# Two scan states multiplied before either is scanned, transposes moved by two steps, small table tiles moved into the mixing phase's memory

## The chip, the cores and the metric

The kernel runs on one core of one Trainium2 chip, in fp32 (matrix products that need the accuracy are made of fp32r pairs, a high part and a low part). The metric is the device time in microseconds (us), the median of the runs shown. Engines are named as in the profile: PE multiplies matrices, DVE is the vector engine, ACT evaluates functions and copies, POOL is the general engine, SP only issues transfers.

## The reference, cut to what matters

```python
for i in range(DEPTH):                                   # DEPTH = 2, SEQ = 256, D_MODEL = 1024
    mod = (cond @ w_ada[i] + b_ada[i])[:, None, :]
    sh1, sc1, g1, sh2, sc2, g2 = jnp.split(mod, 6, axis=-1)
    h = _rmsnorm(x, norm1_g[i]) * (1.0 + sc1) + sh1
    q_a, k_a, v_a, u_s, q_r, k_r, v_r, g_r = jnp.split(h @ w_in[i], split_at, axis=-1)
    y_a = _chunk_band_attention(...)                     # softmax over a band, 8 heads
    y_s = _s5(u_s, ...)                                  # complex diagonal recurrence, below
    y_r = _retention(q_r, k_r, v_r, g_r, ...)            # 4 heads, rotary, group norm
    mixed = jnp.concatenate([y_a, y_s, y_r], axis=-1) @ w_out[i]
    x = x + g1 * mixed
    h = _rmsnorm(x, norm2_g[i]) * (1.0 + sc2) + sh2
    x = x + g2 * _hier_moe(h, ...)                       # 32 gated experts, two per token
return _rmsnorm(x, final_g)

# in _s5
dt = jnp.exp(log_dt)[:, None]
a_bar = jnp.exp(lam * dt)
bu = jnp.einsum('bsgc,gpc->bsgp', ug, b_bar)
_, states = lax.associative_scan(_linear_recurrence_combine, (a_seq, bu), axis=1)
y = jnp.real(jnp.einsum('bsgp,gcp->bsgc', states, c_mat))
```

## The kernel before, in words

Each of the two layers is a mixing phase and an expert phase, and a final norm follows.

**Mixing.** The normed input is transposed on PE (L855), scaled and shifted by the modulation (L863 to L874), and multiplied by the input weights in five products of eight k-chunks (L787 where the result is turned, L792 where it isn't). Each chunk of weights is split into two fp32r parts first: ACT copies the high part (L767), DVE subtracts it for the low part (L768). There are five buffers for split chunks, so ACT and DVE run at most five chunks ahead of PE.

Forty steps run between the chunks of the five products. A table of calls `at(step, ...)` says what each step does besides its chunk. `inner(st)` at steps 2, 10, 18 and 26 makes two states' inputs on PE (L543) in two PSUM banks with the tag `sc`, and DVE takes each state through two multiplications that read the bank (L554, L555), two half-size sums (L556, L557), two scans (L561) and two multiplications into z1 and z2 (L564, L565). The multiplications use a table E per state, which POOL makes in six instructions (L530 to L535). `outer(0)` at step 22 and `outer(1)` at step 35 multiply four states' z1 and z2 on PE (L578). States and tables share 13 buffers (`b`). The `sc` banks also hold retention's scores (L706) and attention's (L624). `ada_slot` spreads the remaining modulation products (L231, L255) over the steps; their rows are finished by DVE sums with a bias (L299 for a full row, L271 for a half row), turned on PE (L309, L285) and copied by DVE (L310, L286). Retention is rotated and normed by DVE; its variance goes through a power on POOL (L335) and three DVE instructions (L337 to L339).

PE's order is the order of the code, POOL's in mixing as well; ACT and DVE are ordered ahead of time by a scheduler that takes dependences and priorities (`high_priority`). Every engine works through its own list in order, so an instruction that waits holds up all behind it.

**The head.** Before the first layer, `s5_prep` makes radius, coefficients and the coarse and fine sine tables from [128, 16] tiles, on DVE with sines on ACT, in a pool of its own (`prep`). ACT squares x for the first norm (L343), then loads its sine table and makes the sines (L418, L419). `rms` scales x by the inverse root (L363 on DVE, L364 on ACT), and the transposes L855 read that.

**Experts.** Weights stream in by DMA through 19 slots of 1 MB; twelve rounds of experts run. `down` multiplies by the last weights (L1325) in two halves of the model width, DVE scales by the gate (L1338), `scatter` puts tokens back on PE (L1356) and DVE adds to x (L1360). In the last round (`end`) each half is scattered as soon as it is made, two token blocks each.

## Time and profile before

| | us |
|---|---|
| three runs | 843.56, 843.98, 847.43 |
| median | 843.98 |
| profiled execution, its own time | 842.86 |
| its span, first to last instruction | 841.1 |
| PE busy in it | 716.7 (85%) |
| DVE busy in it | 499.4 (59%) |
| ACT busy, POOL busy | 252.0 (30%), 112.4 (13%) |
| mean granted TensorE clock | 0.951 |

The profiled execution is the one that all rows below come from; about 1.8 us lie around its span. Busy shares are means over stages of different kinds: in the span's 40 slices of 21 us the transfers run between 413 and 420 GB/s in most slices of the expert phases, and between 141 and 382 GB/s in mixing.

### The profile page before, as it was taken

To read this page: it belongs to the slowest core of one execution; us is meant where nothing else is said; L and a number is where in the kernel's file an instruction comes from. 1 tells how busy PE (TensorE), PEld (TensorE's weight loads), DVE (VectorE), ACT (ScalarE), POOL (GpSimd) and SP (SyncE) were. 2 spreads that over 40 slices of the span, in tenths; PEclk is the share of its full clock that TensorE was granted. 3 is DMA by queue.
4 is the path that set the end of the run, shared out by engine and by line. 5 is a ranking of instruction groups with operands and counts; after the bars stand their busy time and mean duration, and the time that the engine had idled before them with its cause. 6 is when DMAs were issued, how large, how long until landed. Compare 5 with 4: busy or idle time off the path is not lost. (4 is left out here: it accounts for less than half of the span.)

```text
span 841.1 us, 12059 instructions
## 1 busy us (share of the span) xinstructions
PE 716.7 (85%) x4386; PEld 400.6 (48%) x4386; DVE 499.4 (59%) x1146; ACT 252.0 (30%) x541; POOL 112.4 (13%) x165
## 2 busy tenths in 40 slices
PE   3599979899999988598869799689989998869894
PEld 0265757675344443334227478467624344233431
DVE  4689997558555363425359989764865536252533
ACT  2343425934021121111135233394402112111112
POOL 0453160001000000000037215000000000000000
PEclk9599999999999999799999989899999999989998
DMA  9978779898999999999999754659869999989994
GB/s 372 421 269 315 272 284 340 287 376 345 417 420 415 418 416 371 389 409 419 404 413 420 280 168 141 228 216 382 324 216 420 417 415 420 414 334 414 418 411 155
DMA packets 57256, 293.66 MB, mean 349 GB/s; under 512 B 5088, under 2 KB 6880, under 8 KB 33888
## 3 DMA queue, kind: packets, MB, share of 16 engines
q1 hardware_dynamic: 54176, 288.23, 86.5%
q10 hardware_dynamic: 3008, 4.54, 1.6%
q8 instruction: 38, 0.62, 0.3%
q14 instruction: 34, 0.28, 0.1%
HBM read 289.60 MB, written 1.05 MB: 346 GB/s over the span
## 5 line engine op out<-in xcount | busy, mean ns | idle before, releaser
L1297 PE MATMUL mm<-ring,hg 128*32 128x512 f32 (+1 forms) x624 | 108.9, 595 | 0.9 <-DMA ring<-in_wgu_dram 0.9
L767 ACT ACTIVATE wh<-w 128x512 fp32r<-128x512 f32 x120 | 74.5, 630 | 98.8 <-PE mm L792 55.0
L768 DVE TENSOR_TENSOR wh<-w,wh 128x512 fp32r<-128x512 f32 x120 | 85.7, 736 | 28.3 <-ACT wh L767 27.9
L1303 DVE SCALAR_TENSOR_TENSOR b<-mm,cw,b 128x256 f32<-128x256 f32 x24 | 11.6, 483 | 141.2 <-ACT b L1301 141.2
L1297 PE MATMUL mm<-w,hg 128*64 128x512 f32 (+1 forms) x400 | 92.2, 612 | 0.0
L792 PE MATMUL mm<-wh,early 128*128 128x512 f32 x288 | 81.1, 426 | 3.7 <-DVE wh L768 3.6
L1325 PE MATMUL sc<-ring,b 128*64 128x512 f32 (+1 forms) x344 | 69.8, 597 | 1.2 <-ACT b L1311 1.1
L792 PEld LDWEIGHTS mm<-wh,early 128*128 128x128 f32 x288 | 54.7, 200 | 26.3 <-issue 6.6
L1301 ACT ACTIVATE b<-mm 128x256 f32<-128x256 f32 x24 | 9.2, 385 | 172.6 <-PE mm L1297 172.6
L1297 PEld LDWEIGHTS mm<-ring,hg 128*32 128x32 f32 (+1 forms) x624 | 30.9, 119 | 56.6 <-issue 53.3
L1343 ACT ACTIVATE y<-y 128x512 fp32r<-128x512 f32 x44 | 27.7, 629 | 92.4 <-DVE y L1338 92.4
L787 PE MATMUL mm<-early,wh 128*128 128x256 f32 x384 | 51.3, 287 | 2.5 <-DVE wh L768 2.5
L1338 DVE TENSOR_TENSOR y<-sc,gr 128x512 f32<-128x512 f32 x48 | 33.2, 692 | 32.8 <-PE sc L1325 27.0
L1275 POOL TENSOR_TENSOR b<-D,comd 128x128 f32<-128x128 f32 x32 | 12.5, 411 | 292.6 <-PE tr L1280 116.3
L1297 PEld LDWEIGHTS mm<-w,hg 128*64 128x64 f32 (+1 forms) x400 | 27.3, 134 | 50.6 <-issue 49.9
L787 PEld LDWEIGHTS mm<-early,wh 128*128 128x128 f32 x384 | 47.0, 189 | 6.4 <-DVE wh L768 3.0
L1259 PE MATMUL tr<-D,big 128*128 128x256 f32 x192 | 34.7, 323 | 16.8 <-DVE D L1210 15.4
L792 PE MATMUL mm<-wh,big 128*128 128x512 f32 x192 | 47.7, 399 | 1.4 <-DVE y L998 1.4
L231 PE MATMUL ac<-w,cc 128*32 128x512 f32 x192 | 29.1, 691 | 20.3 <-DVE cc L225 10.7
L1259 PEld LDWEIGHTS tr<-D,big 128*128 128x128 f32 x192 | 29.1, 217 | 25.6 <-issue 20.4
L1345 DVE TENSOR_TENSOR y<-y,y 128x512 fp32r<-128x512 f32 x44 | 30.3, 689 | 17.8 <-ACT y L1343 17.5
L792 PEld LDWEIGHTS mm<-wh,big 128*128 128x128 f32 x192 | 35.0, 188 | 9.3 <-DVE y L998 2.2
(367 smaller groups left out, 1161.6 us busy)
## 6 DMA issues: line engine op xcount, KB each, us to landing
ring<-in_wgu_dram SPq DMA_DIRECT2D x78, 1024.0 KB, 16.5
w<-in_wgu_dram SPq DMA_DIRECT2D x50, 1024.0 KB, 14.5
w<-in_w_ada_dram SPq DMA_DIRECT2D x36, 1024.0 KB, 9.1
ring<-in_moe_w_down_dram SPq DMA_DIRECT2D x36, 1024.0 KB, 19.9
w<-in_win_dram SPq DMA_DIRECT2D x22, 1024.0 KB, 7.7
w<-in_moe_w_down_dram SPq DMA_DIRECT2D x20, 1024.0 KB, 17.4
ring<-in_w_ada_dram SPq DMA_DIRECT2D x12, 1024.0 KB, 7.9
w<-in_w_out_dram SPq DMA_DIRECT2D x8, 1024.0 KB, 7.2
```

The source lines that it names most:

```text
L231: PE.matmul(acc[32 * t:32 * t + 32, :], c1[:, k:k + 1].to_broadcast([128, 32]), w[:, t * 512:(t + 1) * 512], start=(k == 0), stop=(k == 7) ...
L767: A.activation(wh[:, 0], w, AF.Copy)
L768: lo_eng[par_[0] % len(lo_eng)].tensor_tensor(wh[:, 1], w, wh[:, 0].bitcast(F32), op=ALU.subtract)
L787: PE.matmul(pt[t][:, f * 256:(f + 1) * 256], whs[i][:, w_, fs], a[x_][:, k], start=first and f + m == 0, stop=end and m == 2, skip_group_c ...
L792: PE.matmul(pt[t], a[x_][:, k, ts_], whs[i][:, w_], start=first and m == 0, stop=end and m == 2)
L1259: PE.matmul(pc[c], (xlo if i else xhi)[:, t, cs], Dm[blk][:, t, ss], start=(i + t == 0), stop=(i + t == 3))
L1275: G.tensor_tensor(Dc[:, t].rearrange("p (e s) -> p e s", s=w), Dm[blk][:, t, po:po + 128].bitcast(F32).rearrange("p (e s) -> p e s", s=w), ...
L1297: PE.matmul(gu[o:o + w, :], hg[blk, k][:, po + o:po + o + w], ws[k // 4][j][:, k % 4] if ahead else part_gu(l, es[j], k), start=(k == 0), ...
L1325: PE.matmul(yp[h][o:o + w, :], aT[:, f * 128 + o:f * 128 + o + w], wd[h][f][j] if ahead else part_wd(l, es[j], f, h), start=(f == 0), stop ...
L1338: V.tensor_tensor(y, yp[h], gates[l, 2][:, h * 512:(h + 1) * 512], op=ALU.mult)
L1343: A.activation(yh, y, AF.Copy)
L1345: V.tensor_tensor(yl, y, yh.bitcast(F32), op=ALU.subtract)
```

## The change

Six edits, the computation is the same:

1. `inner` issues L554 and L555 of both states ahead of either state's scan; `scan` starts from their results.
2. Tables come at step `4*st-6` instead of `4*st-4`. On POOL, whose order is the code's, one thing moves in each layer: the second power of retention (L335) stands behind the table of state 6, where it stood ahead of it.
3. `half_biased` (L285) runs at `g+3` instead of `g+1`, and the sums L271 (of the half row that is turned) and L299 get high priority.
4. `s5_prep` runs in layer 0's mixing phase, its small tiles are slices of one `y2` tile, and an `early` tile that nothing used is gone. `first_squares` copies a column of the cosines into the squares' scratch bank first (one DVE copy more, the only instruction that is new), so ACT's first squares come behind the first sines.
5. `gate_up` gives its activation and product high priority; no instruction changes place by that.
6. In the last round of each layer, the first half's two scatters stand behind the second half's first and second quarter of L1325, where both stood ahead of the second half.

```diff
         def half_slot(l, i):
...
-                V.tensor_tensor(row, acc[:, 0:256], bias_row.pop((l, 2)), op=ALU.add)
+                with tc.high_priority(offset=PRIO):
+                    V.tensor_tensor(row, acc[:, 0:256], bias_row.pop((l, 2)), op=ALU.add)
...
         def ada_gate(l, acc):
...
-            V.tensor_tensor(row, acc, bias_row.pop((l, 1)), op=ALU.add)
+            with tc.high_priority(offset=PRIO):
+                V.tensor_tensor(row, acc, bias_row.pop((l, 1)), op=ALU.add)
...
+        small = []
+
+        def s16():
+
+            if not small:
+                t = y2([128, 512])
+                small.extend(t[:, i * 16:(i + 1) * 16] for i in range(32))
+            return small.pop(0)
...
             sincos(sn, cs, ph, hf)
-            between()
+            between(cs)
...
             def inner(st0):
...
+                ms = []
                 for i, bu in enumerate(bus):
-                    scan(st0 + i, bu)
-
-            def scan(st, bu):
+                    E = E_[st0 + i]
+                    m1 = b2([128, 2, 256])
+                    m2 = b2([128, 2, 256])
+                    with tc.high_priority(offset=PRIO):
+                        V.tensor_tensor(m1, bu, E[:, 0, None, :].to_broadcast([128, 2, 256]), op=ALU.mult)
+                        V.tensor_tensor(m2, bu, E[:, 1, None, :].to_broadcast([128, 2, 256]), op=ALU.mult)
+                    ms.append((m1, m2))
+                for i, m in enumerate(ms):
+                    scan(st0 + i, *m)
+
+            def scan(st, m1, m2):
...
-                        at(4 * st - 4 + i, tables, st + i)
+                        at(max(4 * st - 6, 0) + i, tables, st + i)
...
                     if j == 11:
-                        at(g + 1, lambda: half_biased(l, ada_acc[l, 2]))
+                        at(g + 3, lambda: half_biased(l, ada_acc[l, 2]))
...
-                    if end and (f, j) == (1, len(es) - 1):
-
-                        ys = outputs(yp, True, (h,))
-                        scatter(end, ys, h)
+                    if end and j == len(es) - 1:
+
+                        if f == 1:
+                            ye[h] = outputs(yp, True, (h,))
+                        if h == 1:
+                            scatter(end, ye[0], 0, (f,))
+                            if f == 1:
+                                scatter(end, ye[1], 1)
...
-        with phase("prep"):
-            s5_prep(lambda: all_squares(ss0, ps("mm")))
+
+        def first_squares(cs):
+
+            scr = ps("mm")
+            V.tensor_copy(scr[:, 0:1], cs[:, 0:1])
+            all_squares(ss0, scr)
+
         for l in range(L):
             more = l + 1 < L
             with phase("mix"):
-
-                early()
+                if l == 0:
+                    s5_prep(first_squares)
                 xn = early().rearrange("p (t d) -> p t d", t=2)
```

Line numbers shift by the edit: what stands at L285, L299, L363, L554, L555, L556, L557, L561, L564, L565, L578, L624, L714, L768 and L792 before stands at L286, L301, L365, L562, L563, L571, L572, L576, L579, L580, L593, L639, L729, L783 and L807 in the change.

DVE in the head, before: `early` is the scaled x that the first transposes read, `crs_c` the coarse cosine table, `co_im` a coefficient.

```order
110 L472 TENSOR_TENSOR co_im<-m2t_211,m_36_210 128x16
111 L413 SCALAR_TENSOR_TENSOR b_45_250<-b_46_251,b_45_250 128x256
112 L414 TENSOR_SCALAR b_45_250<-b_45_250 128x256
113 L420 TENSOR_TENSOR b_46_251<-b_46_251 128x256
114 L421 TENSOR_SCALAR crs_c<-b_46_251 128x256
115 L363 TENSOR_SCALAR early_272<-x,rry_280 128x512 x2
```

The same place of the change, up to the scaling of x:

```order
93 L340 SCALAR_TENSOR_TENSOR rrt_248<-rrt_248,ssv_243 128x2
94 L467 TENSOR_TENSOR y_11_111<-y_11_111 128x16
95 L466 SCALAR_TENSOR_TENSOR y_11_111<-y_11_111 128x16
96 L341 SCALAR_TENSOR_TENSOR rry_246<-rrt_248,rry_246 128x2
97 L477 TENSOR_TENSOR y_11_111<-y_11_111,cst 128x16
98 L476 TENSOR_TENSOR y_11_111<-y_11_111,cst 128x16
99 L365 TENSOR_SCALAR early_238<-x,rry_246 128x512 x2
100 L478 TENSOR_TENSOR y_11_111<-y_11_111 128x16
```

The scaling of x stood behind the whole chain of the coarse table and now follows the inverse root (`rry`) at once.

DVE in layer 1, second pair of states, before: `sc` is the bank with a state's input, `y<-ac,bad` the sum L299 of a modulation row, `y<-sc,cst` retention's masked scores.

```order
890 L554 TENSOR_TENSOR b_1837_6604<-sc_6598,b_1809_6494 128x512
891 L555 TENSOR_TENSOR b_1838_6605<-sc_6598,b_1809_6494 128x512
892 L299 TENSOR_TENSOR y_1851_6668<-ac_6210,bad_6211 128x512
893 L556 TENSOR_TENSOR b_1837_6604<-b_1837_6604,b_1838_6605 128x256
894 L557 TENSOR_TENSOR b_1837_6604<-b_1837_6604,b_1838_6605 128x256
895 L310 COPY modT_96<-tr_6695 128x16
896 L561 SCALAR_TENSOR_TENSOR b_1838_6605<-radius,b_1837_6604 128x256 x2
897 L564 TENSOR_TENSOR b_1839_6612<-b_1838_6605,b_1809_6494 128x512
898 L554 TENSOR_TENSOR b_1840_6615<-sc_6599,b_1813_6509 128x512
899 L555 TENSOR_TENSOR b_1841_6616<-sc_6599,b_1813_6509 128x512
```

The same pair in the change:

```order
888 L562 TENSOR_TENSOR b_1807_6569<-sc_6563,b_1775_6433 128x512
889 L563 TENSOR_TENSOR b_1808_6570<-sc_6563,b_1775_6433 128x512
890 L562 TENSOR_TENSOR b_1809_6573<-sc_6564,b_1780_6457 128x512
891 L563 TENSOR_TENSOR b_1810_6574<-sc_6564,b_1780_6457 128x512
892 L301 TENSOR_TENSOR y_1824_6642<-ac_6175,bad_6176 128x512
893 L571 TENSOR_TENSOR b_1807_6569<-b_1807_6569,b_1808_6570 128x256
```

The second bank is read two rows behind the first instead of eight, and the sum of the row stands two full-size multiplications later.

PE in layer 1 near the end of the products, before: `tr<-cst,y` is the turning of the half row, `mm<-wh,early` the products, `sc<-b,b` attention's first scores, `ac<-b,par` and `ac<-b,b` are `outer(1)`.

```order
2086 L792 MATMUL mm_7207<-wh_7231,early_6279 128x512
2087 L285 MATMUL tr_7240<-cst,y_1942_7229 128x128 x2
2088 L792 MATMUL mm_7206<-wh_7244,early_6278 128x512 x2
2089 L792 MATMUL mm_7206<-wh_7244,early_6279 128x512
2090 L792 MATMUL mm_7207<-wh_7244,early_6278 128x512 x2
...
2092 L624 MATMUL sc_7253<-b_1789_6407,b_1788_6406 128x256
```

The change, at the end of `outer(1)`, which stands behind those scores:

```order
2112 L593 MATMUL ac_6929<-b_1856_6812,par_6190 32x256
2113 L593 MATMUL ac_6929<-b_1890_7040,par_6190 32x256
2114 L593 MATMUL ac_6929<-b_1892_7044,par_6190 32x256
2115 L286 MATMUL tr_7265<-cst,y_1912_7194 128x128 x2
2116 L807 MATMUL mm_7171<-wh_7271,early_6243 128x512 x2
```

The turning moved behind two chunks of the last product, the scores and `outer(1)`. In layer 0 it moved less: behind 18 products (L787) and one turning of retention (L748 twice).

## Rows read from the trace of the kernel before

**Rows 1.** The page: busy time by engine, and transfer rate in 40 slices.

```profile
PE 716.7 (85%) x4386; PEld 400.6 (48%) x4386; DVE 499.4 (59%) x1146; ACT 252.0 (30%) x541; POOL 112.4 (13%) x165
...
GB/s 372 421 269 315 272 284 340 287 376 345 417 420 415 418 416 371 389 409 419 404 413 420 280 168 141 228 216 382 324 216 420 417 415 420 414 334 414 418 411 155
```

**Rows 2.** Windows, layer 1: busy PE, PEld, DVE, ACT, POOL; PEclk, DMA share, GB/s.

```profile
480.00:490.00 10.00, 6.59 (x22) 4.82 (x23) 9.82 (x18) 1.38 (x4) 5.87 (x8) 0.75 0.55 207
...
500.00:510.00 10.00, 10.00 (x111) 8.23 (x108) 8.52 (x26) 2.18 (x5) 2.82 (x4) 1.00 0.53 184
510.00:520.00 10.00, 9.51 (x75) 8.61 (x75) 10.00 (x16) 4.88 (x8) 8.64 (x10) 1.00 0.49 150
```

**Rows 3.** Timeline of PE, the head: start, duration, work, [idle before <- releaser].

```profile
24.88 1.93 PE L231 MATMUL ac<-w,cc 128*32 128x512 f32 x8 [0.55 <-DMA w<-in_w_ada_dram]
29.68 1.97 PE L855 MATMUL sc<-cst,early 128*128 128x128 f32 x8 [2.87 <-DVE early L363]
```

**Rows 4.** Timeline of DVE, the head.

```profile
20.45 0.15 DVE L339 SCALAR_TENSOR_TENSOR rry<-rrt,rry 128x2 f32<-128x2 f32 x1
...
28.69 1.71 DVE L363 TENSOR_SCALAR early<-x,rry 128x512 f32<-128x512 f32 x2
```

**Rows 5.** Timeline of PE and of DVE, layer 0 near the half row.

```profile
116.81 1.57 PE L787 MATMUL mm<-early,wh 128*128 128x256 f32 x11 [1.98 <-DVE wh L768]
...
125.05 0.44 PE L285 MATMUL tr<-cst,y 128*128 128x128 f32 x2 [2.98 <-DVE y L271]
...
124.57 0.42 DVE L271 TENSOR_TENSOR y<-ac,bad 128x256 f32<-128x256 f32 x1
```

**Rows 6.** Timeline of PE and of DVE, layer 1, second pair of states.

```profile
485.36 1.64 PE L706 MATMUL sc<-y,y 64*128 64x256 f32 x6 [3.10 <-DVE b L555]
486.94 5.29 PE L792 MATMUL mm<-wh,early 128*128 128x512 f32 x12
...
484.63 0.68 DVE L555 TENSOR_TENSOR b<-sc,b 128x512 f32<-128x512 f32 x1
```

**Rows 7.** Timeline of PE and of DVE, layer 1, end of the scans.

```profile
532.12 1.42 PE L792 MATMUL mm<-wh,early 128*128 128x512 f32 x5 [0.77 <-DVE wh L768]
539.02 0.69 PE L285 MATMUL tr<-cst,y 128*128 128x128 f32 x2 [5.48 <-DVE y L271]
539.36 2.91 PE L792 MATMUL mm<-wh,early 128*128 128x512 f32 x6
542.20 1.32 PE L624 MATMUL sc<-b,b 64*128 64x256 f32 x8
...
545.04 1.07 PE L578 MATMUL ac<-b,par 128*32 128x256 f32 x16
...
537.95 0.68 DVE L565 TENSOR_TENSOR b<-b,b 128x512 f32<-128x512 f32 x1
```

**Rows 8.** Timeline of POOL and of DVE, layer 1, table of state 6.

```profile
508.20 1.11 POOL L335 TENSOR_TENSOR rvy<-rvar,mhalf 128x4 f32<-128x4 f32 x1 [5.71 <-DVE rvar L735]
509.28 0.62 POOL L530 TENSOR_TENSOR b<-crs_c,fine_c 128x256 f32<-128x256 f32 x1
...
513.86 0.99 POOL L535 TENSOR_TENSOR b<-b,b 128x256 f32<-128x256 f32 x1
...
509.34 0.57 DVE L337 TENSOR_TENSOR rvt<-rvy 128x4 f32<-128x4 f32 x1 [0.90 <-POOL rvy L335]
...
517.02 1.11 DVE L768 TENSOR_TENSOR wh<-w,wh 128x512 fp32r<-128x512 f32 x1
```

**Rows 9.** Timeline of PE, end of layer 0, start and end of layer 1.

```profile
437.90 1.94 PE L855 MATMUL sc<-cst,early 128*128 128x128 f32 x8 [1.47 <-DVE early L363]
...
825.18 1.98 PE L1356 MATMUL ac<-y,sT 128*128 128x512 f32 x4 [0.81 <-DVE y L1338]
827.09 1.92 PE L1325 MATMUL sc<-ring,b 128*32 128x512 f32 x16
829.90 1.98 PE L1356 MATMUL tr<-y,sT 128*128 128x512 f32 x4 [0.89 <-DVE y L1338]
```

More of the change, by code (lines that the diff above doesn't have):

```diff
@@ L373, in body @@
         COEF = [1.0 / 5040, 1.0 / 720, 1.0 / 120, 1.0 / 24, 1.0 / 6, 0.5, 1.0]
+        small = []
[4 more added lines that the diff above has]
+            return small.pop(0)
         def expm1(src, w, tag):
-            xx = sb([128, w], tag + "x")
+            xx = s16()
             V.tensor_scalar(xx, src, -87.3, 88.0, op0=ALU.max, op1=ALU.min)
-            n = sb([128, w], tag + "n")
+            n = s16()
             round_(n, xx, 1.4426950408889634)
@@ L382, in expm1 @@
             V.scalar_tensor_tensor(xx, n, -LN2L, xx, op0=ALU.mult, op1=ALU.add)
-            q = sb([128, w], tag + "q")
+            q = s16()
             V.tensor_scalar(q, xx, 1.0 / 40320, COEF[0], op0=ALU.mult, op1=ALU.add)
@@ L392, in expm1 @@
             p2 = ni.bitcast(F32)
-            em1 = sb([128, w], tag + "em1")
+            em1 = s16()
             V.tensor_tensor(em1, q, p2, op=ALU.mult)
-            pm1 = sb([128, w], tag + "pm1")
+            pm1 = s16()
             V.tensor_scalar(pm1, p2, -1.0, None, op0=ALU.add)
             V.tensor_tensor(em1, em1, pm1, op=ALU.add)
-            ex = sb([128, w], tag + "ex")
+            ex = s16()
             V.tensor_scalar(ex, q, 1.0, None, op0=ALU.add)
@@ L433, in s5_prep @@
             _, dt = expm1(ldt, 16, "e1")
-            live = sb([128, 16], "live")
+            live = s16()
             V.tensor_scalar(live, ldt, -87.3, None, op0=ALU.is_ge)
             V.tensor_tensor(dt, dt, live, op=ALU.mult)
-            zr = sb([128, 16], "zr")
+            zr = s16()
             V.tensor_tensor(zr, C("are"), dt, op=ALU.mult)
-            phi = sb([128, 16], "phi")
+            phi = s16()
             V.tensor_tensor(phi, C("aim"), dt, op=ALU.mult)
-            n = sb([128, 16], "pn")
-            ph = sb([128, 16], "ph")
+            n = s16()
+            ph = s16()
             mod2pi(ph, phi, n)
@@ L445, in s5_prep @@
             V.tensor_copy(radius, ex)
-            sn = sb([128, 16], "psn")
-            cs = sb([128, 16], "pcs")
-            hf = sb([128, 16], "phf")
+            sn = s16()
+            cs = s16()
+            hf = s16()
             sincos(sn, cs, ph, hf)
-            between()
-            nr = sb([128, 16], "nr")
-            ni = sb([128, 16], "nni")
+            between(cs)
+            nr = s16()
+            ni = s16()
             V.tensor_tensor(nr, em1, cs, op=ALU.mult)
@@ L456, in s5_prep @@
             V.tensor_tensor(ni, ex, sn, op=ALU.mult)
-            m2 = sb([128, 16], "m2")
-            t = sb([128, 16], "m2t")
+            m2 = s16()
+            t = s16()
             V.tensor_tensor(m2, C("are"), C("are"), op=ALU.mult)
@@ L463, in s5_prep @@
             V.reciprocal(m2, m2)
-            t2 = sb([128, 16], "m2t2")
+            t2 = s16()
             V.tensor_tensor(t, nr, C("are"), op=ALU.mult)
@@ L472, in s5_prep @@
             V.tensor_tensor(co_im, t, m2, op=ALU.mult)
-            ph16 = sb([128, 16], "ph16")
+            ph16 = s16()
             V.tensor_scalar(phi, ph, 16.0, None, op0=ALU.mult)
             mod2pi(ph16, phi, n)
-            t16 = sb([128, 16], "t16")
+            t16 = s16()
             V.tensor_scalar(t16, C("iota")[:, 0:16], -1.0, None, op0=ALU.add)
@@ L544, in inner @@
                                   tile_position=(o, 0))
+                ms = []
                 for i, bu in enumerate(bus):
-                    scan(st0 + i, bu)
-            def scan(st, bu):
+                    E = E_[st0 + i]
[8 more added lines that the diff above has]
+            def scan(st, m1, m2):
                 q = l * 8 + st
                 E = E_.pop(st)
-                m1 = b2([128, 2, 256])
-                m2 = b2([128, 2, 256])
-                with tc.high_priority(offset=PRIO):
-                    V.tensor_tensor(m1, bu, E[:, 0, None, :].to_broadcast([128, 2, 256]), op=ALU.mult)
-                    V.tensor_tensor(m2, bu, E[:, 1, None, :].to_broadcast([128, 2, 256]), op=ALU.mult)
                 V.tensor_tensor(m1[:, 0], m1[:, 0], m2[:, 1], op=ALU.subtract)
@@ L1299, in gate_up @@
                               start=(k == 0), stop=(k == 7), tile_position=(0, o))
-                si = b1_([128, 256])
-                A.activation(si, gu[:, 0:256], AF.Silu)
-                act = b1_([128, 256])
-                V.scalar_tensor_tensor(act, gu[:, 256:512], cw, si, op0=ALU.mult, op1=ALU.mult)
+                si, act = b1_([128, 256]), b1_([128, 256])
+                with tc.high_priority(offset=PRIO):
+                    A.activation(si, gu[:, 0:256], AF.Silu)
+                    V.scalar_tensor_tensor(act, gu[:, 256:512], cw, si, op0=ALU.mult, op1=ALU.mult)
                 return act
@@ L1315, in down @@
                 _, _, w, _, _, es = rounds[r]
-                yp = [ps("sc") for _ in range(2)]
+                yp, ye = [ps("sc") for _ in range(2)], {}
                 if ahead and end:
@@ L1347, in outputs, with scatter @@
                 return out
-            def scatter(sT, ys, h0=0):
+            def scatter(sT, ys, h0=0, ts=(0, 1)):
                 for h, (yh, yl) in enumerate(ys, h0):
                     hs = slice(h * 512, (h + 1) * 512)
-                    for t in range(2):
+                    for t in ts:
                         p = ps(("ac", "tr")[h])
```

## The prediction

> **What bounds the kernel now.** I read the page first. PE is busy for 85% of the span and DVE for 59% [rows 1], but these shares mix stages, so the transfer rate in 40 slices comes next: it stands at 413 to 420 GB/s through most of the expert phases and falls to 141 to 382 in mixing [rows 1]. The expert phases go at the pace of the weights; mixing doesn't. The windows of layer 1's mixing show what it goes by: from 500 to 510 us PE is busy for all of 10.00 us, from 510 to 520 DVE is, and from 480 to 490 DVE is busy for 9.82 while PE has 6.59 and a granted clock of 0.75 [rows 2]. So PE and DVE take turns, and a microsecond is to be had only where PE stands still for DVE. The timeline of PE names these places. In the head PE waits 2.87 us for the scaled x [rows 3]. In layer 0 it waits 1.98 and 2.98 us [rows 5], in layer 1 3.10 us [rows 6], 0.77 and 5.48 us [rows 7]. At the end two scatters lie between the halves of the last round [rows 9].
>
> What is saved in mixing should reach the end, since the expert phases' transfers start as slots and routing allow, not by a clock of their own: in the two slices from 589 to 631 us, around the end of layer 1's mixing, the rate is 324 and 216 [rows 1], so transfers wait there for the core.
>
> **The head (term A).** Before, DVE had the inverse root of the norm by 20.60 (20.45 + 0.15) but scaled x only at 28.69, behind the chain of the coarse cosines [rows 4]. Now the scaling follows the root. What is late next is PE itself: the modulation product that stands ahead of the transposes ends at 26.81 (24.88 + 1.93) [rows 3]. The transposes go from 29.68 to about 26.85: **A = 2.8 us**. The squares now come behind the first sines and the one new copy. Even if they pushed the root back by 4 us, the scaling (1.71) would end at 20.60 + 4 + 1.71 = 26.3, ahead of 26.85; so that costs nothing, and each microsecond beyond 4.5 would cost one. POOL's tables get their coarse tables later by at most the scaling's 1.71 from a chain that otherwise starts earlier, and nobody waits for them in the head.
>
> **Layer 0's mixing (B0).** The half row's turning waited 2.98 us for its sum at 124.57 [rows 5]. The turning now stands 18 products and two transposes later; 11 products took 1.57 [rows 5], so 18 take about 2.6, and even with the sum no earlier the wait would be 0.4. The 1.98 ahead of it is a wait for a split chunk (L768) behind a state's multiplications and scan. DVE has no less work, only another order, so this may return at the next chunk. Bounds: 2.6 us if all of it returns, 4.96 if none does. **B0 = 3.3**, nearer the lower end, since DVE is fully busy there as in the like window of layer 1 (10.00 of 10) [rows 2].
>
> **Layer 1's mixing (B1).** Two places. The first: retention's scores need a bank that the second state's L555 frees; that ended at 485.31 (484.63 + 0.68), and PE waited 3.10 for it [rows 6]. Now the bank is read two rows behind the first one, and that wait goes. The sum L299 falls behind two multiplications more of 0.68 each [rows 6], so the turning L309 waits up to 1.4 more. Net 1.7. The 12 products behind it took 5.29 us, at a mean clock of 0.75, a mix of its two levels of 1.2 and 2.4 GHz [rows 2, 6]; six at the full clock take 1.7 (1.42 for five) [rows 7], so 12 take 3.4, and up to 1.9 more comes back if the clock stays up.
>
> The second: the turning that waited 5.48 now stands behind `outer(1)`. It can't wait again, as the sum it needs stands in DVE's list ahead of the last state's L565, which `outer(1)` needs. What is late next is that L565: it ended at 538.63 (537.95 + 0.68), while `outer(1)` began at 545.04 [rows 7]. PE, let go at 533.54 (532.12 + 1.42), has 12 products (3.4) and the scores (1.32) to do: 538.3 [rows 7]. Both allow a start near 539.2 with some queueing, 5.8 earlier, even if DVE is not a microsecond ahead of before. The slow 2.91 for six products after the stall [rows 7] is part of these 5.8.
>
> The 1.7 (or 3.6) of the first place helps the second only if DVE gets ahead too, and from 510 to 520 it has no idle time [rows 2] but for what came before: 0.90 us behind POOL's power [rows 8]. So of the first place I keep 0.5. **B1 = 6.3**. Bounds: 3, if the splits of the last product come later by half of the stall; 9.4, if the first place passes whole (5.8 + 3.6).
>
> **The ends (C0, C1).** In layer 1 the second half's products started at 827.09, behind the first half's scatters, and its own scatter at 829.90 [rows 9]. Now the first eight products run while DVE scales the first half (PE waited 0.81 for that [rows 9]); one scatter block (0.99) stands ahead of the second eight and one behind. PE's own work is unchanged (1.92 + 1.98 until the last scatter), so it gains its wait of 0.81 and the wait of 0.89 at 829.90 that the other block now covers: **C1 = 1.5**, at most 1.7, at least 0.8. The same edit in layer 0 can only shorten the wait of 1.47 for the scaled x at 437.90 [rows 9], where the transfers of the modulation weights set the pace otherwise: **C0 = 0.4** of 0 to 1.47.
>
> **What costs nothing.** POOL's order changes only at retention's second power, which now stands behind a table of 5.6 us (509.28 to 514.85) [rows 8]. The table waits for buffers of `outer(0)`, the power for the table, DVE's L337 for the power, and behind L337 stand splits that PE needs. But DVE's list has 13 instructions between the variance and L337 where it had one; six are full-size at up to 0.68 [rows 7], four are scans, which I put at the same, and three half-size, at half: 7.8, which covers the table and the power of 1.11 [rows 8] with 1 us to spare. The high priority in the expert rounds moves nothing. The memory of the small tiles takes away a wait at most.
>
> **Sum.** 2.8 + 3.3 + 6.3 + 1.5 + 0.4 = 14.3 us. The profiled execution took 842.86, so 828.6; the median of the runs is 1.1 above it, 843.98, so I forecast **829.7 us**.
>
> **Rivals.**
>
> *The waits come back as waits for splits.* DVE's work is the same, and it has windows without idle time [rows 2]; PE then only waits elsewhere. Against it: in layer 1 `outer(1)` stood 6.4 us behind the DVE result that it needs (545.04 less 538.63) [rows 7], and that is not DVE's work. Half of B0 and B1 lost gives 829.7 + 4.8 = 834.5; all but A, C1 and the 2.6 of B0 lost gives 843.98 - 6.9 = 837.1.
>
> *Layer 0's saving is lost in the transfers.* If weights for the first expert phase arrive no earlier, A and B0 vanish: 829.7 + 6.1 = 835.8. For it speaks that the rate is 376 and 345 in the slices from 168 to 210 us [rows 1], against it that these are below the 417 to 420 of the slices that follow.
>
> *POOL in DVE's way.* A split that ran beside the table took 1.11 us (517.02) where DVE's other full-size instructions there take 0.68 [rows 7, 8]. The table of 5.6 us starts about 1.1 earlier now, as the power no longer stands ahead of it. Were it and the next one, in both layers, moved whole from idle to busy DVE time, that would be 5 instructions of 0.43 more each per table, 2.2, and 8.6 over four: 838.3. I see only 1.1 us of shift, so this is unlikely. The Trainium skill says it as a rule (GPSIMD Engine Reference, Key points): POOL shares its SBUF interfaces with the vector engine and contends with vector instructions that have two SBUF inputs. The trace's 1.11 agrees.
>
> *Slower: POOL's power holds DVE.* If `outer(0)` comes late, because PE itself waits for splits, the table, the power and L337 slip with it, and DVE stops with the splits behind L337. Each microsecond by which `outer(0)` slips past the 1 us of cover costs one in each layer. It eats the whole gain when the slip is 14.3 / 2 + 1 = 8.2 us; a slip of 10 gives 829.7 + 18 = 847.7. Against it: PE was busy for 10.00 of 10 us around `outer(0)` in layer 1 [rows 2], so nothing made it late.
>
> **How the numbers follow.** My forecast, 825 to 834, gets 0.70; the waits that come back, 834 to 838, 0.13; lost in the transfers 0.06; POOL in the way 0.03; no gain at all for a cause I don't see 0.04; slower 0.04. The lower end takes the upper bounds of B0, B1 and C1 together in part (4.96 + 9.4 + 1.7 + 2.8 + 0.4 = 19.3 gives 824.7, and all at once is unlikely); the upper end takes in the rivals that still gain: 825 to 839. Half a per cent, about what can be told from no change, is 4.2 us, so faster means under 839.8: 0.70 + 0.13 + 0.06 and nearly all of POOL's 0.03 make 0.91, and I take 0.89 as the cases' own ends reach over. Same 0.07, slower 0.04.
>
> **What would show it.** In the changed profile: the first transposes near 26.9 us behind a modulation product, with no wait for DVE (A); no wait at the half row's turning in either layer, and `outer(1)` of layer 1 within 1 us of the last L565 (B0, B1); no wait at retention's scores, and a longer one at L309 in layer 1; a last scatter about 1.5 us nearer to the second half's first product. Wrong it would be if the windows of 10 us show PE's waits for L768 grown by what the others lost, if DVE waits several microseconds for POOL's second power, or if the first weights of the expert phases land as late as before.

## The result and the profile after

The changed kernel took 823.83 us, median of four runs (822.90 to 825.42), beside 843.81 before: the ratio is 0.9768, with a 95% interval of 0.9746 to 0.9789, so about 20 us or 2.3% less. The forecast was 829.7 with a range down to 825.0: the side was right, the size 30% short, and the time lies below the range.

The page of the changed kernel, lines as in [rows 1]; its span is 821.1 us:

```profile
PE 711.6 (87%) x4386; PEld 397.6 (48%) x4386; DVE 491.4 (60%) x1147; ACT 251.8 (31%) x541; POOL 114.4 (14%) x165
...
GB/s 369 420 371 303 291 344 291 295 335 416 414 422 414 419 416 359 399 412 417 406 409 420 336 189 145 288 259 316 300 314 421 415 417 418 401 350 412 419 410 154
```

Most slices of the expert phases stand at the rates that they had before, and most of the 20 us is gained in the head and in mixing. To see where, one follows PE through both traces: its list is the same but for a few places, so the start of one instruction before, less its start after, is the lead that the change has at that place.

| place on PE | before | after | lead | forecast of the step |
|---|---|---|---|---|
| first scan inputs, layer 0 (L543) | 54.78 | 49.46 | 5.3 | A, 2.8 |
| third scan inputs, layer 0 (L543) | 95.68 | 87.84 | 7.8 | none (it was 2.5) |
| attention's first scores, layer 0 (L624) | 139.31 | 132.39 | 6.9 | B0, 3.3 (0.9 lost since the row above, 1.6 in all) |
| first turning of the scans' input matrices, layer 1 (L504) | 448.74 | 440.27 | 8.5 | C0, 0.4 (it was 1.5) |
| retention's first turning, layer 1 (L695) | 474.96 | 463.60 | 11.4 | none (it was 2.9) |
| `outer(0)`, layer 1 (L578) | 506.86 | 493.32 | 13.5 | 0.5 of B1 (2.2 since the row above, 5.1 in all) |
| `outer(1)`, layer 1 (L578) | 545.04 | 523.39 | 21.7 | 5.8 of B1 (it was 8.1) |
| first expert round's turning, layer 1 (L1309) | 616.89 | 597.11 | 19.8 | none (1.9 given back) |
| end of the span | 841.1 | 821.1 | 20.0 | C1, 1.5 (it was 0.2) |

The head, PE (compare [rows 3]); columns of every timeline below are start, duration, work and [idle before <- releaser], lines of the code as in the changed kernel:

```profile
24.73 1.68 PE L231 MATMUL ac<-w,cc 128*32 128x512 f32 x8 [0.55 <-DMA w<-in_w_ada_dram]
26.33 1.09 PE L870 MATMUL sc<-cst,early 128*128 128x128 f32 x8
27.26 0.60 PE L870 MATMUL tr<-cst,early 128*128 128x128 f32 x4
27.70 0.60 PE L870 MATMUL mm<-cst,early 128*128 128x128 f32 x4
```

The transposes follow the modulation product with no wait, as forecast. What was not forecast: the first eight take 1.09 us where they took 1.97.

Layer 0, retention's first scores and the bank that they wait for, PE of the kernel before and then of the changed kernel:

```profile
81.56 1.71 PE L706 MATMUL sc<-y,y 64*128 64x256 f32 x8
```

```profile
75.57 0.92 PE L721 MATMUL sc<-y,y 64*128 64x256 f32 x8
```

This is the place of [rows 6], one layer earlier. Before, the bank came free with DVE's L555 at 82.24 (81.56 and 0.68), in the middle of the eight. The next scores went from 1.41, with a wait of 0.54 ahead of them, to 0.92, and a wait of 0.61 for a split (at 71.57) went too. Together that is about the 2.5 of the table. It is edit 1's: with edit 1 alone both groups of scores take 0.92, in the whole without it 1.71 and 1.40.

Layer 0 near the half row, PE and DVE (compare [rows 5]):

```profile
115.84 0.44 PE L286 MATMUL tr<-cst,y 128*128 128x128 f32 x2 [0.98 <-DVE y L272]
...
119.47 0.69 PE L763 MATMUL tr<-cst,b 128*128 128x128 f32 x2 [2.19 <-DVE big L769]
119.81 6.12 PE L802 MATMUL mm<-early,wh 128*128 128x256 f32 x30
...
115.38 0.41 DVE L272 TENSOR_TENSOR y<-ac,bad 128x256 f32<-128x256 f32 x1
```

The wait of 1.98 fell to 0.19 (at 107.23) and that of 2.98 to 0.98, and one of 2.19 came where none was: retention's second turning (L763) needs the bank that DVE's L769 reads, and the half row's turning now stands between the two and holds the other bank. The 30 products behind it took 6.12 us; before they took 3.84.

The granted clock stands beside both places in the windows (columns as in [rows 2]; the third column from the end is the clock, 1.00 being 2.4 GHz and 0.50 being 1.2). The kernel before, the head's transposes and the 30 products:

```profile
31.00:32.00 1.00, 1.00 (x7) 1.00 (x6) 0.00 (x0) 0.00 (x0) 0.94 (x2) 0.50 1.00 418
...
119.00:122.00 3.00, 3.00 (x34) 1.95 (x30) 3.00 (x6) 0.05 (x1) 0.00 (x0) 1.00 0.85 307
```

The changed kernel, the same two:

```profile
27.00:28.00 1.00, 1.00 (x11) 1.00 (x10) 0.00 (x0) 0.00 (x0) 1.00 (x2) 1.00 0.98 410
...
120.00:123.00 3.00, 3.00 (x16) 3.00 (x16) 3.00 (x9) 1.39 (x4) 0.00 (x0) 0.50 1.03 415
```

The head came up from the lower level to the upper one, and the products near the half row went the other way.

Layer 1, second pair of states, PE (compare [rows 6]):

```profile
471.00 1.09 PE L311 MATMUL tr<-cst,y 128*128 128x128 f32 x4 [3.13 <-DVE y L301]
471.74 1.63 PE L807 MATMUL mm<-wh,early 128*128 128x512 f32 x3
473.30 1.65 PE L721 MATMUL sc<-y,y 64*128 64x256 f32 x8
474.88 3.81 PE L807 MATMUL mm<-wh,early 128*128 128x512 f32 x12
```

The scores no longer wait for their bank, and the row's turning waits 3.13 in place of 1.08. The 12 products behind take 3.81 in place of 5.29.

Just ahead of this, before and then after:

```profile
469.48 1.43 PE L792 MATMUL mm<-wh,early 128*128 128x512 f32 x5 [1.85 <-DVE wh L768]
...
472.37 2.75 PE L792 MATMUL mm<-wh,early 128*128 128x512 f32 x6
```

```profile
459.67 1.44 PE L807 MATMUL mm<-wh,early 128*128 128x512 f32 x5 [0.55 <-DVE wh L783]
...
462.10 1.66 PE L807 MATMUL mm<-wh,early 128*128 128x512 f32 x6
```

A wait for a split fell by 1.30, and the scan inputs and the six products behind it took 1.13 and 1.66 in place of 1.60 and 2.75. That makes about the 2.9 of the table. The wait goes with edit 1: it is 0.54 with edit 1 alone, and 1.85 in the whole without it.

Layer 1, end of the scans, PE and DVE (compare [rows 7]):

```profile
521.80 1.66 PE L807 MATMUL mm<-wh,early 128*128 128x512 f32 x6
523.39 1.10 PE L593 MATMUL ac<-b,par 128*32 128x256 f32 x15
...
525.50 0.44 PE L286 MATMUL tr<-cst,y 128*128 128x128 f32 x2
...
523.35 0.68 DVE L580 TENSOR_TENSOR b<-b,b 128x512 f32<-128x512 f32 x1
```

Here `outer(1)` runs right at the last state's L580 (L565 before): that ends at 524.03, 14.6 us earlier than before, and PE no longer stands 6.4 us behind it.

### The profile page after: what moved, and what is told of

The parts are those of the page before. It is cut to its first block, busy times and chain, and to the rows that moved or that the text cites. A ratio compares the mean times of both kernels' runs of the same rounds, so it can differ in the third digit from the quotient of the medians.

```text
span 821.1 us, 12064 instructions
## 1 busy us (share of the span) xinstructions
PE 711.6 (87%) x4386; PEld 397.6 (48%) x4386; DVE 491.4 (60%) x1147; ACT 251.8 (31%) x541; POOL 114.4 (14%) x165
## 5 line engine op out<-in xcount | busy, mean ns | idle before, releaser
L783 DVE TENSOR_TENSOR wh<-w,wh 128x512 fp32r<-128x512 f32 x120 | 85.2, 733 | 25.4 <-ACT wh L782 24.9
L807 PE MATMUL mm<-wh,early 128*128 128x512 f32 x288 | 77.3, 411 | 0.9 <-DVE wh L783 0.9
L807 PEld LDWEIGHTS mm<-wh,early 128*128 128x128 f32 x288 | 52.4, 192 | 22.0 <-issue 6.3
L802 PE MATMUL mm<-early,wh 128*128 128x256 f32 x384 | 53.2, 295 | 1.6 <-DVE wh L783 1.6
L802 PEld LDWEIGHTS mm<-early,wh 128*128 128x128 f32 x384 | 49.3, 198 | 5.4 <-DVE wh L783 2.0
L807 PE MATMUL mm<-wh,big 128*128 128x512 f32 x192 | 47.6, 398 | 1.4 <-DVE y L1013 1.4
L807 PEld LDWEIGHTS mm<-wh,big 128*128 128x128 f32 x192 | 35.0, 188 | 9.2 <-DVE y L1013 2.2
## 6 DMA issues: line engine op xcount, KB each, us to landing
w<-in_wgu_dram SPq DMA_DIRECT2D x50, 1024.0 KB, 14.3
```

The source lines that it names most:

```text
L783: lo_eng[par_[0] % len(lo_eng)].tensor_tensor(wh[:, 1], w, wh[:, 0].bitcast(F32), op=ALU.subtract)
L802: PE.matmul(pt[t][:, f * 256:(f + 1) * 256], whs[i][:, w_, fs], a[x_][:, k], start=first and f + m == 0, stop=end and m == 2, skip_group_c ...
L807: PE.matmul(pt[t], a[x_][:, k, ts_], whs[i][:, w_], start=first and m == 0, stop=end and m == 2)
```

## The experiments

Each was timed beside runs of the kernel before on the same chip. Gains in us are (1 - ratio) times 843.8, so 19.6 for the whole change.

| kernel | median, us | ratio (95% interval) | gain, us |
|---|---|---|---|
| before + 4 (head) | 837.47 | 0.9939 (0.9917 to 0.9960) | 5.1 |
| before + 1 (multiplications ahead) | 848.94 | 1.0067 (1.0049 to 1.0085) | -5.7 |
| before + 3 (turning later, row sums first) | 838.96 | 0.9957 (0.9943 to 0.9972) | 3.6 |
| before + 6 (last round) | 842.47 | 0.9990 (0.9971 to 1.0010) | 0.8, not told from none |
| before + 1 + priority of L299 | 841.38 | 0.9968 (0.9953 to 0.9983) | 2.7 |
| before + 1 + 3 | 832.06 | 0.9864 (0.9849 to 0.9879) | 11.5 |
| before + matmuls of no use in the head | 844.99 | 1.0015 (0.9998 to 1.0032) | -1.3, not told from none |
| after - 1 | 832.51 | 0.9867 (0.9842 to 0.9892) | 11.2 |
| after - priority of L299 | 829.91 | 0.9830 (0.9812 to 0.9848) | 14.3 |
| after - 2 (tables at the old steps) | 827.22 | 0.9812 (0.9797 to 0.9826) | 15.9 |
| after + two turnings later | 820.52 | 0.9714 (0.9692 to 0.9737) | 24.1 |
| after + retention's second turning later | 818.87 | 0.9704 (0.9687 to 0.9720) | 25.0 |

**The head alone.** Edit 4 was put into the kernel before, with the small tiles that it needs; its core:

```diff
-        with phase("prep"):
-            s5_prep(lambda: all_squares(ss0, ps("mm")))
...
-                early()
+                if l == 0:
+                    s5_prep(first_squares)
```

> The kernel before with edit 4 alone (small tiles in the mixing phase, first squares behind the first sines). Theory from the two traces: the head gains the wait of 2.8 us and about 2.4 more because PE's clock is at its upper level for the transposes, so 5 us in all: 838.8. Rival, as the prediction has it: only the wait, 2.8: 841.0. Rival, lost later in transfers or in waits for DVE: 843.8, no change.

It gained 5.1 us: the wait and the clock. In its trace PE is 4.3 ahead at the first scan inputs (54.78 to 50.53) and 6.3 at the end (841.1 to 834.8), so the rival that it is lost in the transfers falls.

**Multiplications ahead, alone.** Edit 1 was put into the kernel before, with nothing else:

```diff
-                    scan(st0 + i, bu)
...
+                    ms.append((m1, m2))
+                for i, m in enumerate(ms):
+                    scan(st0 + i, *m)
```

> The kernel before with edit 1 alone (both states' first multiplications ahead of either scan). Theory: the wait at retention's scores in layer 1 goes, the clock stays up and DVE follows, 4 to 5 us: 839. Rival, as the prediction has it: DVE has no idle time at the end of the scans, so only 0.5 of it stays: 843.3. In both the turning of the half row in layer 1 still waits, 5 us or more.

Neither: it is slower by 5.7 us. In its trace the wait at the scores is gone, and the turning of the full row waits, PE of layer 1:

```profile
478.47 0.94 PE L796 MATMUL mm<-wh,early 128*128 128x512 f32 x3
488.95 1.08 PE L309 MATMUL tr<-cst,y 128*128 128x128 f32 x4 [9.54 <-DVE y L299]
```

With both states' multiplications first, the sum L299, which has no priority there, falls behind both states' scans on DVE. In layer 0 the edit alone loses too: the half row's turning waits 4.20 (2.98 before) and a split 2.78 (1.98 before).

**Turning later and row sums first, alone.** Edit 3 was put into the kernel before, the two priorities (of L271 and L299) and the later step:

```diff
-                        at(g + 1, lambda: half_biased(l, ada_acc[l, 2]))
+                        at(g + 3, lambda: half_biased(l, ada_acc[l, 2]))
```

> The kernel before with edit 3 alone (the half row turned two steps later, the two row sums at high priority). Theory from the traces: layer 1's turning gives 8, with the slow products behind it, less 2 given back in attention, layer 0 gives 1 to 2: 836.5. Rival, as the prediction has it: 5.8 and 2.6, 835.4. Rival, the edit is worth something only with edit 1: under 3 us, 841 or more.

It gained 3.6, between the theories. The turnings of the half row wait no more than 0.30 us in layer 0 and not at all in layer 1, but the scores still wait 2.60 and retention's second turning of layer 0 waits 2.6.

**The last round alone.** Edit 6 was put into the kernel before:

```diff
+                        if f == 1:
+                            ye[h] = outputs(yp, True, (h,))
+                        if h == 1:
+                            scatter(end, ye[0], 0, (f,))
```

> The kernel before with edit 6 alone (the last rounds' scatters between the quarters). Theory from the trace: the last weights land when they did, and the last scatter stands 3.1 us behind them where it stood 3.4: 0.3 to 0.5, 843.4. Rival, as the prediction has it: 1.5 and 0.4, 841.9.

0.8 us with an interval over zero. The trace of the changed kernel shows what it ends on. Windows of half a microsecond, before and then after; the last three columns are PE clock, DMA share and GB/s:

```profile
826.50:827.00 0.50, 0.50 (x2) 0.00 (x0) 0.50 (x1) 0.00 (x0) 0.00 (x0) 1.00 0.15 57
827.00:827.50 0.50, 0.50 (x5) 0.16 (x8) 0.47 (x2) 0.38 (x1) 0.00 (x0) 1.00 0.00 0
```

```profile
806.50:807.00 0.50, 0.50 (x2) 0.00 (x0) 0.00 (x0) 0.00 (x0) 0.00 (x0) 1.00 0.24 90
807.00:807.50 0.50, 0.50 (x4) 0.15 (x6) 0.19 (x1) 0.00 (x0) 0.00 (x0) 1.00 0.04 16
```

```profile
807.20 1.55 PE L1340 MATMUL sc<-ring,b 128*32 128x512 f32 x8
808.68 1.12 PE L1375 MATMUL ac<-y,sT 128*128 128x512 f32 x2
809.64 1.88 PE L1375 MATMUL tr<-y,sT 128*128 128x512 f32 x4
```

Before, the second half's products began at 827.09, just as the last weights were in (827.0); their transfer had hidden behind the scatters. After, the last eight products begin at 807.20, again just as the last weights are in (807.2). So it is the weights that set this place in both, and only the work behind them is shorter: the last scatter starts 2.4 us behind the end of the transfers (809.64 less 807.2) where it was 2.9 (829.90 less 827.0).

**The whole without edit 1.** Each state's scan stands behind its own multiplications again:

```diff
-                for i, m in enumerate(ms):
-                    scan(st0 + i, *m)
+                    scan(st0 + i, bu)
```

> The changed kernel without edit 1 (each state's scan behind its own multiplications again). Theory: edit 1 is worth much once the row sums have priority, since then the bank is free early and the sum isn't late: without it the single edits add up to 843.8 - 5.1 - 3.6 - 0.8, about 834. Rival, as the prediction has it: little of edit 1 stays, 825 to 826.

832.51: with the others in place, edit 1 is worth 8.4 us (19.6 less 11.2). Alone it cost 5.7.

**Edit 1 with one priority.** To the kernel before:

```diff
+            with tc.high_priority(offset=PRIO):
-            V.tensor_tensor(row, acc, bias_row.pop((l, 1)), op=ALU.add)
+                V.tensor_tensor(row, acc, bias_row.pop((l, 1)), op=ALU.add)
```

> The kernel before with edit 1 and the high priority of the full row's sum L299 alone. Theory: what made edit 1 alone slower by 5.7 us is that this sum falls behind both states' scans, so that the turning L309 waits 9.5 us in layer 1; with the priority it waits about 3, and edit 1 then gains its 3 to 5 at the scores and the clock: 841 to 843. Rival: the loss is the half row's or the buffers', 848.

841.38: these two lines turn edit 1 from 5.7 slower to 2.7 faster. The full row's turning waits 3.13 in layer 1. In layer 0 the half row's turning, whose sum has no priority here, still waits 4.55.

**Matmuls of no use in the head.** They were put on PE between the modulation products and ahead of the transposes of the kernel before.

```diff
+                    hot = ps("ac")
                     for k in range(7):
                         ada_mm(acc0, k, ada0[k])
+                        for _ in range((0, 0, 0, 1, 1, 1, 5)[k]):
+                            PE.matmul(hot[:, 0:256], ident, cst[:, 0:256], start=True, stop=True)
```

> The kernel before with eight matmuls of no use in the head, which keep PE busy between the modulation products and up to the first transposes; nothing else is moved and no result changes. Theory: 2.4 of the head's 5.3 us are the clock, so the transposes (1.97, 1.06, 1.06) take 1.09, 0.60 and 0.60 and the product behind them 1.06 of 1.62, 2.2 us in all: 841.6. Rival: the upper level was chance, or PE falls behind by these matmuls: 843.8 or more.

The end is no earlier, but the rows tell the two questions apart, PE and then DVE:

```profile
25.64 2.42 PE L840 MATMUL ac<-cst 128*128 128x256 f32 x10
29.82 1.09 PE L858 MATMUL sc<-cst,early 128*128 128x128 f32 x8 [1.76 <-DVE early L363]
30.75 0.60 PE L858 MATMUL tr<-cst,early 128*128 128x128 f32 x4
31.18 0.60 PE L858 MATMUL mm<-cst,early 128*128 128x128 f32 x4
...
42.24 0.80 PE L885 MATMUL mm<-early,wh 128*128 128x256 f32 x2 [8.09 <-ACT early L876]
...
33.99 4.08 DVE L768 TENSOR_TENSOR wh<-w,wh 128x512 fp32r<-128x512 f32 x4 [3.47 <-ACT wh L767]
38.00 0.16 DVE L317 TENSOR_TENSOR modT<-tr,cst 128x16 f32<-128x16 f32 x1
```

The transposes take 1.09, 0.60 and 0.60 as in the changed kernel, although x still comes late, and the next turning (L316) starts 3.68 us behind them, where it was 5.96. The clock there, in a window of this kernel:

```profile
30.00:31.00 1.00, 1.00 (x11) 1.00 (x11) 0.53 (x1) 0.22 (x1) 0.92 (x2) 1.00 1.02 424
```

So 2.3 us there are the clock. They were lost behind it: with the matmuls in PE's list the scheduler put the four splits L768 ahead of the modulation on DVE, and the first product waits 8.09. As a test of the end time it is confounded.

**Two turnings later.** The changed kernel with

```diff
-                        at(g + 1, lambda: ada_biased(l, 1, ada_acc[l, 1]))
+                        at(g + 1 + 2 * l, lambda: ada_biased(l, 1, ada_acc[l, 1]))
...
-                at(29, rout, 1)
+                at(32, rout, 1)
```

> The changed kernel with two turnings moved: the full row's of layer 1 by two steps (it waited 3.13 us for its sum) and retention's second by three (2.19 in layer 0, and 30 products behind it took 6.12 us of 3.84). Theory: both waits go and the clock stays up, 3 to 6 us: 819. Rival: DVE has no idle time there and PE waits for splits in their place: 823.

820.52. In layer 1 its lead over the changed kernel is 5.4 at `outer(0)` (493.32 to 487.97), and 1.1 at `outer(1)` (523.39 to 522.31); it had 1.5 when layer 1 began (445.58 to 444.04). So there all that layer 1 had added was lost again, in one new wait on PE, for a bank that ACT frees; ACT's list is shown behind it:

```profile
497.01 7.31 PE L802 MATMUL mm<-early,wh 128*128 128x256 f32 x36 [3.22 <-ACT b L967]
...
496.06 0.42 ACT L755 ACTIVATE b<-r 128x256 f32<-128x256 f32 x1 [8.77 <-DVE rvar L749]
```

L967, which frees the bank, stands right behind L755 on ACT, and L755 waited 8.77 us for retention's variance on DVE (2.87 in the changed kernel). From 490 to 500 us of this kernel DVE is busy for 10.00 of 10. So PE had got ahead of DVE, and waited for it by way of ACT.

**Retention's second turning alone.** The changed kernel with

```diff
-                at(29, rout, 1)
+                at(32, rout, 1)
```

> The changed kernel with only retention's second turning moved by three steps. Theory: in layer 0 the wait of 2.19 and the slow 30 products behind it go, 4 us, and this is nearly all of what the two moves together gave, as layer 1's lead of 5 was down to 1 at the second outer product: 820 to 821. Rival: the lead of layer 0 doesn't reach the end, and the gain was layer 1's: 823.

818.87, the lowest median here, though its interval overlaps with that of the two moves together. The 30 products of layer 0 take 3.85 again, and nothing waits at L763:

```profile
117.34 3.85 PE L802 MATMUL mm<-early,wh 128*128 128x256 f32 x30
...
123.61 0.38 PE L763 MATMUL tr<-cst,b 128*128 128x128 f32 x2
```

**Edits 1 and 3, nothing else.** The kernel before with both of the diffs above.

> The kernel before with edits 1 and 3 together and nothing else. Theory: the two need each other, so together they give what of the changed kernel's 20 us the head (5.1) and the last round (0.8) leave: about 830. Rival, each is worth what it is alone (5.7 slower, 3.6 faster): 846.

832.06: 11.5 us, where the two alone give 3.6 - 5.7 = -2.1. So 13.6 of the change's 19.6 us are in the pair and in neither one. In its trace the half row's turning of layer 0 waits no more, which had waited 4.20 with edit 1 alone.

**The whole without the priority of L299.**

```diff
-            with tc.high_priority(offset=PRIO):
-                V.tensor_tensor(row, acc, bias_row.pop((l, 1)), op=ALU.add)
+            V.tensor_tensor(row, acc, bias_row.pop((l, 1)), op=ALU.add)
```

> The changed kernel without the high priority of the full row's sum L299 alone. Theory: the sum falls behind both states' scans, the turning L309 of layer 1 waits 8 to 10 us where it waits 3.1, and PE's products behind it are slow: 830 to 832. Rival: the lead is taken back by DVE's full list at the end of the scans in any case, so little is lost: 824 to 825.

829.91, 5.3 us lost. PE waits 9.6 us at the full row's turning in layer 1.

**The whole with the tables at their old steps.**

```diff
-                        at(max(4 * st - 6, 0) + i, tables, st + i)
+                        at(4 * st - 4 + i, tables, st + i)
```

> The changed kernel with the tables at their old steps, so that retention's second power stands ahead of the table of state 6 again. As the prediction has it, the earlier tables cost and bring nothing: 823 to 825. Rival: the power behind the table holds DVE up, so that this is faster, 821. Rival: the earlier table is what lets the third pair of states start, 827 or more.

827.22, so edit 2 is worth 3.7 us and didn't cost nothing or bring nothing. In layer 0, DVE and then PE of this kernel:

```profile
99.95 0.58 DVE L339 TENSOR_TENSOR rvt<-rvy 128x4 f32<-128x4 f32 x1 [0.90 <-POOL rvy L337]
...
110.07 1.74 DVE L783 TENSOR_TENSOR wh<-w,wh 128x512 fp32r<-128x512 f32 x2
...
111.27 2.72 PE L802 MATMUL mm<-early,wh 128*128 128x256 f32 x11 [2.76 <-DVE wh L783]
113.91 2.08 PE L554 MATMUL sc<-uT,bT 32*128 32x256 f32 x8
117.78 4.46 PE L802 MATMUL mm<-early,wh 128*128 128x256 f32 x24
```

With the power ahead of the table, DVE's list has retention's norm early again: it waits 0.90 for POOL, takes the norm and the scans, and the splits come at 110.07 (105.95 in the changed kernel). PE waits 2.76 (0.19 in the changed kernel), and then runs at half rate: 11 products take 2.72 (1.58), 24 take 4.46 (3.14). A window of that stretch:

```profile
112.00:114.00 2.00, 2.00 (x12) 1.78 (x10) 1.97 (x4) 0.00 (x0) 0.00 (x0) 0.50 0.55 92
```

Part of this loss comes back at once: retention's second turning, which waited 2.19 in the changed kernel, doesn't wait here, and the 30 products behind it take 3.83 (6.12). The 3.7 us are what is left.

## Why the prediction was too small

**A, the head: right mechanism, mis-sized.** 2.8 was forecast, 5.3 came, and 5.1 by edit 4 alone. The term took the transposes' old durations along. They had run at PE's lower clock, and 2.3 of the 2.5 us that are missing are that, as the matmuls of no use show. How much comes back varies from run to run: in kernels with edit 4 the turning behind them starts at 29.65, 29.91, 29.97, 30.01, 30.73, 31.27 and 31.29, all with the same order of work on PE up to there.

**B0, layer 0: 1.6 of 3.3, and not from where it was forecast.** 2.5 came at a place that the prediction doesn't name, the scores and a split ahead of them (see the second row of the table of leads). At the places that it does name, the waits of 1.98 and 2.98 became 0.19 and 0.98. I wrote that one "may return at the next chunk"; what came was a wait at retention's turning for a PSUM bank, 2.19, and behind it a slow clock worth 2.3 (6.12 against 3.84). Edit 3 made room for it, since the half row's turning stands between the two others in the ring of two banks: with edit 3 alone the same turning waits 2.64. It is not there in every kernel with edit 3: with edits 1 and 3, and in the whole without edit 2, PE had already waited 2.80 and 2.76 for splits ahead of it. Moving the second turning by three steps removes both, and some 5 us more are gained in all. I had read this ring in the order of the change and not in the waits it makes.

**B1, layer 1: 11.3 of 6.3, the step that failed.** It failed in two ways. The first is the sentence that of the first place "I keep 0.5", because DVE "has no idle time". The window from which I took that begins at 510 us. Between 500 and 510 DVE was busy for 8.52 of 10 [rows 2], and from 490 to 500 for 7.21:

```profile
490.00:500.00 10.00, 10.00 (x78) 8.12 (x78) 7.21 (x16) 4.47 (x9) 0.00 (x0) 0.91 0.48 148
```

What it waited for there were ACT's copies of chunks (L767) and PE's turning (L721), so with PE earlier the scans' work could begin earlier, and did. Two windows of the changed kernel (columns as in [rows 2]):

```profile
480.00:490.00 10.00, 10.00 (x91) 8.78 (x91) 9.00 (x22) 2.57 (x6) 2.06 (x3) 1.00 0.75 233
490.00:500.00 10.00, 10.00 (x108) 8.41 (x107) 10.00 (x25) 4.37 (x8) 4.92 (x7) 1.00 0.32 105
```

All of the lead of 13.5 at `outer(0)` arrived at `outer(1)`. The last state's L580 ends 14.6 us earlier, of which 8.5 were there when layer 1 began: DVE got 6.1 ahead within layer 1 where I had allowed 0.5. The second place added 8.1: the wait of 5.48, 0.77 ahead of it, and the slow products and scores behind it (2.91 to 1.63 for six, 1.32 to 0.92). Some 1.9 of this was given back in attention. The limit that I saw is there, only later: the kernel with two turnings moved got 3.8 us further ahead at `outer(0)` and kept none of it.

The second is that edit 1 was costed at one place only, the scores of layer 1's second pair of states. That place gave 2.2 (1.7 to 3.6 was the forecast, before the 0.5). But the edit acts on every pair of both layers: the wait for a split ahead of that pair's inputs and the slow rows behind it gave 2.9 in layer 1, and the like places of layer 0 gave the 2.5 above. Both stand in the trace of the kernel before, and both are put at nothing. Together they are 5.4 us, nearly the 5.7 by which the sum of 14.3 fell short of 20.0; the other misses, up and down, about cancel.

**The sum over edits.** I costed edits by places, and not by all the places where they act. I also didn't see that edit 1 by itself loses: my net of 3.10 less 1.4 took the sum L299 at its place in the order of the change, where edit 3's priority holds it. Nowhere did I ask what edit 1 does without that.

**Edit 2: costs nothing, it said; it is worth 3.7.** I priced it as a risk: POOL's power later, DVE waiting. The later power did not hold DVE up (L339 follows at 107.10 in layer 0 and 507.08 in layer 1, with no idle time); between the variance and L339 stand 14 instructions in layer 0 and 12 in layer 1, three of these scans, where I counted 13 with four. It made the scheduler put retention's norm behind the splits that PE needs. That DVE's work is the same held for its instructions, not for its busy time, which fell from 499.4 to 491.4 us; no run separates the reasons.

The Trainium skill (GPSIMD Engine Reference, Key points) has the rule that POOL shares its SBUF interfaces with the vector engine and contends with instructions that have two SBUF inputs. The changed kernel's trace agrees (a split L783 takes 1.22 us at 105.95 beside POOL's table, and 0.68 at 109.91 at the table's end). The loss of up to 8.6 us that the rival put on it did not come.

**C0 and C1: 1.5 of 0.4, and 0.2 of 1.5.** C1's step failed where I counted PE's waits of 0.81 and 0.89 as gain; behind them stood the landing of the last weights, at 827.0 and 807.2. C0's wait was not shortened (1.57 after, 1.47 before). Where its lead comes from is open: it was 8.7 at layer 0's second expert round (230.69 to 222.03, where 17 products took 4.08 us in place of 5.77), 4.6 in the ninth (365.96 to 361.34), 6.8 at the last round's products (419.68 to 412.89) and 8.5 at its last scatter (427.15 to 418.64). The last 1.7 stand where edit 6 acts, but in the kernel with edit 6 alone it is 0.5 there, and these are single executions.

**Rivals.** That the waits come back as waits for splits held only where edit 1 is in and edit 2 is not: in layer 0 PE waits 2.78 us for a split with edit 1 alone, 2.80 with edits 1 and 3, and 2.76 in the whole without edit 2, where it waited 1.98 before. With both it waits 0.19 there, and in layer 1 a wait of 0.49 grew to 1.36. Layer 0's saving was not lost in the transfers. The slower case did not occur, but a slower change was near: edit 1 alone.

**Open.** The head's clock varies by 1.6 us between runs, and no run here shows what sets it.

## What to carry to other kernels

An edit that brings work forward on an engine that works in order pushes something back: look for the small instruction (here a sum of 0.68 us) that another engine waits for, and give it priority in the same edit; here it turns 5.7 us slower into 2.7 faster, and with the half row's sum first and its turning later into 11.5. Cost an edit at every place where its code runs, and not only where the wait is longest: the two places left out here were worth 5.4 us. Count a stall on PE with the instructions behind it, at the duration that the same work has elsewhere in the trace. Before calling an engine full, look at the window ahead of the full one: idle time there is where the work will go.

## What was not expected of the hardware

PE's clock made a good part of the size. Behind a stall of 2.19 us the 30 products of layer 0 took 6.12 us in place of 3.84, a loss as large as the stall. Behind one of 2.76, in the whole without edit 2, 11 products, the eight L554, a modulation product and 24 products lost 4.3 together (the eight L554 alone 2.08 in place of 1.13), more than the stall; behind one of 3.13 a turning, 15 products and the scores lost 2.6 (12 products 3.81, 3.06 in layer 0). But with edit 3 alone the wait at retention's second turning was 2.64 and the 30 products behind it took 3.81, and a wait of about 1 us (L286 in layer 0) was followed by rows at full rate. So stalls of like length cost differently, even at the same place: in these rows a stall removed gives back between one and two and a half times its length.
